# Layer 1's first expert: its rows by products from blocks on chip, its tables inside the first expert, and the overflow branch at each layer's end

## The chip, the cores and the metric

One core of a Trainium2 chip runs the kernel. The metric is device time in microseconds (us) of one execution. Engines: TensorE (PE, matrix products), VectorE (DVE), ScalarE (ACT), GpSimd (POOL) and SyncE (SP, which here issues loads).

## The reference

Two layers over 512 rows of width 1024. After a mixer and memory attention, each layer ends with an output projection, a norm and a grouped top-2 mixture of 16 experts:

```python
o = jnp.concatenate([tok, xa], axis=-1) @ w_out[i]
x = layer_norm(ALPHA * x + o, ln1_g[i], ln1_b[i])
f = grouped_moe(x, router_w, router_b, w_gate[i], w_up[i], w_down[i])
x = layer_norm(ALPHA * x + f, ln2_g[i], ln2_b[i])
...
scores = jax.nn.sigmoid(jnp.dot(xt.astype(jnp.float32), router_w.astype(jnp.float32)))
sel = scores + router_b.astype(jnp.float32)
...
for e in range(N_EXPERTS):
    h = jax.nn.silu(xt @ w_gate[e]) * (xt @ w_up[e])
    out = out + combine[:, e:e + 1] * (h @ w_down[e])
```

The group of four experts with the best sum of its two best `sel` is taken for each row, and in it the two best experts; `combine` holds their scores divided by their sum, and zero elsewhere.

## The kernel before

The 512 rows are four blocks of 128 (`xrow[0]` to `xrow[3]`, each 128 x 1024 on chip). Every large product is done as three (`mm3`, L202 to L204: high by high, high by low, low by high), so each operand is split into a high part, copied by ScalarE (L168), and a low part, a subtraction on VectorE (L169) or now and then on POOL. Weights come in pages of 1 MB through `W`: SP loads a raw page, the splits make high and low, and PE uses them; `W.keep`, `W.ahead` and `W.on_pool` say how many pages stay free, how far splits run ahead, and which of them POOL does.

The stage around the change, for each layer, is this. The output projection (`project_out`, products `oa`) is done column by column, one row block each, and each block goes through its norm (L458 to L466). `logits` stores the normed block to `x1d` and `rd` in HBM by POOL's queue, transposes it (products `rt`) and multiplies it with the router's weights (`lg`). `route` is a chain of some twenty small VectorE operations for blocks 0 to 2 together and then for block 3: ranks in the groups, the chosen group, `oh` (which experts a row goes to), and its place within each expert's list, which comes from PE counts (`pos`). With comparisons `sel` (0/1 matrices of 128 x 128, row by slot) `entries` multiplies a table `tok` of row numbers and gate factors into slots (`tab`); `tables` turns that into `idxs` (row number of each of 128 slots of each of 16 experts) and `gates`. `overflow` counts what doesn't fit in 128 slots (`cnt`, `ovf`, `nover`).

`experts` then gathers the rows of expert 0 and 1 from `x1d` by an indirect DMA of POOL (`xg`, L668), warms PE up (layer 1 only), runs `fill` (in layer 0 the keys and values of layer 1, `ka` and `va`, which hide the wait), and at `more` every engine loads `nover` (L893) and branches (L894) past the rare code for overfull experts. Then for each expert: transposes of the gathered rows (`xt`, split to `xgt`), `gate_up` (48 products `ga` and `ua` in two halves), an activation and a product (`h`), its transposes (`htr`, split to `ht`), and `down` (24 products `ya`), scaled by the gate and scattered into `rd`. Within the experts the order on PE, ScalarE and VectorE is that of the code (`manual_schedule`); before them, and at the last expert until its warm-up, a scheduler orders by its own costs. At the layer's end eight warm-up products, htr, four more, and the last expert's `ya` follow, whose result is added with `rd` for the second norm.

## Time and profile before

| | |
|---|---|
| median of three runs | 1035.75 us (1032.32 to 1035.86) |
| the profiled execution's own time | 1031.97 us, span 1030.1 us |
| mean granted TensorE clock | 0.973 |
| PE busy | 983.7 us, 95% of the span |
| VectorE, ScalarE, POOL busy | 774.2, 627.7, 200.5 us |
| time per expert in the steady part | 17.9 us |

The span goes from the first to the last instruction. PE is the engine that is busy nearly throughout; its idle stretches lie where a layer's experts begin. A granted clock of 1 is 2.4 GHz, 0.5 is 1.2 GHz.

### The profile page before, as it was taken

To read this page: it belongs to the slowest core of one execution; us is meant where nothing else is said; L and a number is where in the kernel's file an instruction comes from. 1 tells how busy PE (TensorE), PEld (TensorE's weight loads), DVE (VectorE), ACT (ScalarE), POOL (GpSimd) and SP (SyncE) were. 2 spreads that over 40 slices of the span, in tenths; PEclk is the share of its full clock that TensorE was granted. 3 is DMA by queue.
4 is the path that set the end of the run, shared out by engine and by line. 5 is a ranking of instruction groups with operands and counts; after the bars stand their busy time and mean duration, and the time that the engine had idled before them with its cause. 6 is when DMAs were issued, how large, how long until landed. Compare 5 with 4: busy or idle time off the path is not lost. (4 is left out here: it accounts for less than half of the span.)

```text
span 1030.1 us, 12721 instructions
## 1 busy us (share of the span) xinstructions
PE 983.7 (95%) x4815; PEld 810.6 (79%) x4816; DVE 774.2 (75%) x884; ACT 627.7 (61%) x684; POOL 200.5 (19%) x111
## 2 busy tenths in 40 slices
PE   8999999969999999999999999977899999999995
PEld 6788888858888888888679887865688888888873
DVE  4738567867989898898894455675689898988975
ACT  4626532556788787878643414233687887878763
POOL 0000002112332413321110000221133324233023
PEclk9999999989999999999999999987899999999998
DMA  9813266667999999999880425490799999999944
GB/s 321 294 42 123 91 237 247 244 225 265 364 367 333 366 360 360 360 357 362 282 320 1 164 82 207 131 396 25 232 330 362 372 327 383 359 362 355 357 87 160
DMA packets 102219, 273.30 MB, mean 265 GB/s; under 512 B 10442, under 2 KB 10966, under 8 KB 102152
## 3 DMA queue, kind: packets, MB, share of 16 engines
q1 hardware_dynamic: 89480, 242.84, 64.5%
q0 software_dynamic: 11808, 26.97, 9.4%
q10 hardware_dynamic: 864, 2.62, 0.7%
q8 instruction: 39, 0.64, 0.2%
q14 instruction: 28, 0.23, 0.1%
HBM read 262.22 MB, written 26.21 MB: 280 GB/s over the span
## 5 line engine op out<-in xcount | busy, mean ns | idle before, releaser
L169 DVE TENSOR_TENSOR low<-raw,high 128x2048 fp32r<-128x2048 f32 x189 | 427.9, 2288 | 80.9 <-ACT high L168 79.4
L168 ACT ACTIVATE high<-raw 128x2048 fp32r<-128x2048 f32 x189 | 355.1, 1910 | 22.7 <-PE ga L204 10.1
L668 POOL DMA_INDIRECT xg<-x1d,idxs x32 | 83.2, 2601 | 299.6 <-PE xt L677 270.5
L168 ACT ACTIVATE split<-raw 128x1024 fp32r<-128x1024 f32 x66 | 68.9, 1058 | 71.1 <-PE za L204 26.0
L202 PE MATMUL ya<-high,ht 128*128 128x512 f32 x256 | 103.8, 406 | 0.0
L169 DVE TENSOR_TENSOR split<-raw,split 128x1024 fp32r<-128x1024 f32 x61 | 73.6, 1221 | 39.6 <-ACT split L168 38.9
L204 PE MATMUL ga<-high,xgt 128*128 128x512 f32 x248 | 99.1, 399 | 2.9 <-DVE xgt L208 2.9
L204 PE MATMUL ya<-high,ht 128*128 128x512 f32 x256 | 101.3, 396 | 0.1
L203 PE MATMUL ya<-low,ht 128*128 128x512 f32 x256 | 101.1, 395 | 0.0
L202 PE MATMUL ga<-high,xgt 128*128 128x512 f32 x248 | 100.7, 406 | 0.1
L203 PE MATMUL ga<-low,xgt 128*128 128x512 f32 x248 | 98.4, 397 | 0.0
L204 PE MATMUL ua<-high,xgt 128*128 128x512 f32 x248 | 97.1, 392 | 0.0
L202 PE MATMUL ua<-high,xgt 128*128 128x512 f32 x248 | 96.9, 391 | 0.0
L203 PE MATMUL ua<-low,xgt 128*128 128x512 f32 x248 | 96.8, 390 | 0.0
L169 POOL TENSOR_TENSOR split<-raw,split 128x1024 fp32r<-128x1024 f32 x5 | 11.9, 2383 | 267.0 <-DVE sto L475 147.0
L202 PE MATMUL za<-xh,split 128*128 128x512 f32 x160 | 61.6, 391 | 2.0 <-ACT xh L207 2.0
L203 PE MATMUL za<-xl,split 128*128 128x512 f32 x160 | 62.5, 391 | 0.0
L204 PE MATMUL za<-xh,split 128*128 128x512 f32 x160 | 61.5, 389 | 0.0
L204 PEld LDWEIGHTS ga<-high,xgt 128*128 128x128 f32 x248 | 47.4, 191 | 14.1 <-DVE xgt L208 4.0
L204 PEld LDWEIGHTS ya<-high,ht 128*128 128x128 f32 x256 | 48.1, 188 | 12.8 <-DVE ht L208 1.3
L664 POOL DMA_INDIRECT rd<-h,idxs x16 | 40.4, 2523 | 89.3 <-ACT h L718 79.6
L202 PEld LDWEIGHTS ya<-high,ht 128*128 128x128 f32 x256 | 48.4, 189 | 10.5 <-ACT ht L207 0.6
(250 smaller groups left out, 1886.2 us busy)
## 6 DMA issues: line engine op xcount, KB each, us to landing
raw<-in_w_gate_dram SPq DMA_DIRECT2D x64, 1024.0 KB, 9.8
raw<-in_w_up_dram SPq DMA_DIRECT2D x64, 1024.0 KB, 9.6
raw<-in_w_down_dram SPq DMA_DIRECT2D x64, 1024.0 KB, 10.5
raw<-in_w_kv_dram SPq DMA_DIRECT2D x8, 1024.0 KB, 7.4
raw<-in_w_out_dram SPq DMA_DIRECT2D x8, 1024.0 KB, 8.0
raw<-in_w_in_b_dram SPq DMA_DIRECT2D x8, 1024.0 KB, 11.1
raw<-in_w_in_a_dram SPq DMA_DIRECT2D x6, 1024.0 KB, 5.4
x1d<-x POOLq DMA_DIRECT2D x8, 512.0 KB, 6.0
```

The lines of the kernel that those rows point to most:

```text
L168: act.activation(high, src, AF.Copy)
L169: (pool_e if self.on_pool(self.count) else vec).tensor_tensor(low, src, high, op=OP.subtract)
L202: pe.matmul(o, a[0], b[0], start=start, stop=False)
L203: pe.matmul(o, a[0], b[1], start=False, stop=False)
L204: return pe.matmul(o, a[1], b[0], start=False, stop=stop)
L664: added[e] = pool_e.indirect_dma_start(out=rd[i], out_offset=bass.IndirectOffsetOnAxis(ap=tabs[e][0], axis=0), in_=ys[e % 2], in_offset=No ...
L668: pool_e.indirect_dma_start(out=xg[:, e % 2], out_offset=None, in_=x1d[i], in_offset=bass.IndirectOffsetOnAxis(ap=tabs[e][0], axis=0), bou ...
```

## The change

Layer 0: the routing is cut into steps of a class (`choose`, `both`, `count`, `place`, `places`, `gates`). The lists of rows (`listed`, which makes `idxs`) are made apart from the gate factors (`weighed`). The two gathers are begun in the midst of the V products of `keys_values`, whose last half is put behind the list's last product. The gate factors and the overflow count (`rest`) follow, and the transposes of expert 0 come after the last V product.

Layer 1 (`mixer_end_dense`) has one written order from the output projection on. Expert 0 needs no list: 0/1 matrices `sel0` (row by slot of expert 0) are multiplied with the row blocks on chip (`first_rows`, 32 products `x0`), which gives its rows transposed. Four half pages of weights are split early and the others held back. The tables (`listed`, the gathers for experts 1 and 2) come after the first 12 products of expert 0, gate factors and overflow after the next 12. The norm of the last block is done in two halves, and the warm-up before the experts is gone.

Both layers: `more` (L958, L959) stands at the last expert, between its `gate_up` and the warm-up products, with a page of its own; one more page is kept free.

```diff
-    def keys_values(after=None):
+    def keys_values(begin=None):
...
         a = [acc("va") for _ in range(2)]
         for j in range(4):
+            if j == 2 and begin is not None:
+                begin()
             g = W.next()
             for kk in range(2):
                 k = 2 * j + kk
                 for m in range(2):
                     ms = slice(m * P, (m + 1) * P)
-                    with ExitStack() if after is None or j < 3 else tc.issue_after(after):
-                        mm3(a[m], (memh[:, k, ms], meml[:, k, ms]), (g[:, 0, kk, :], g[:, 1, kk, :]),
-                            k == 0, k == KB - 1)
+                    with ExitStack() if begin is None or j < 2 else tc.issue_after(last_listed[0]):
+                        end = mm3(a[m], (memh[:, k, ms], meml[:, k, ms]), (g[:, 0, kk, :], g[:, 1, kk, :]),
+                                  k == 0, k == KB - 1)
             W.done(g)
...
+        return kt, vt, end.ins
...
-    def entries(cs):
-
+    def chosen(sels=None, cs=range(NC)):
+
+        sels = page("sels", [P, NC, 2, P], FR) if sels is None else sels
         for c in cs:
-            if c == 0:
-                tab[:] = [tiny(3 * E, "tab")]
             for k in range(2):
-                m = pe.matmul(tab[0], choose(pos2[:, k, c:c + 1]), tok[:, c, k].rearrange("p e t -> p (e t)"),
-                              start=(c + k == 0), stop=(c + k == NC))
-        last_entry.append(m.ins)
-
-    def tables():
-
-        t = tab[0].rearrange("p (e t) -> p e t", t=3)
-        vec.tensor_scalar(idxs, t[:, :, 0], 1.0, None, op0=OP.subtract)
-        return vec.tensor_reduce(gates, t[:, :, 1:3], axis=AX.X, op=OP.add)
+                vec.tensor_scalar(sels[:, c, k], slot1, pos2[:, k, c:c + 1], None, op0=OP.is_equal)
+        return sels
+
+    def listed(sels, t=None, cs=range(NC)):
+
+        t = tiny(E, "rows") if t is None else t
+        for c in cs:
+            for k in range(2):
+                m = pe.matmul(t, sels[:, c, k], tok[:, c, k, :, 0], start=(c + k == 0), stop=(c + k == NC))
+        if NC - 1 in cs:
+            vec.tensor_scalar(idxs, t, 1.0, None, op0=OP.subtract)
+            last_listed[:] = [m.ins]
+        return t
+
+    last_listed = []
+
+    def weighed(sels):
+
+        t = tiny(2 * E, "gates").rearrange("p (e t) -> p e t", t=2)
+        for c in range(NC):
+            for k in range(2):
+                pe.matmul(t, sels[:, c, k], tok[:, c, k, :, 1:3], start=(c + k == 0), stop=(c + k == NC))
+        vec.tensor_reduce(gates, t, axis=AX.X, op=OP.add)
+        drop(sels)
 
...
-        def gate_up(e, between=None):
+        def gate_up(e, between=None, then=()):
             a = [acc("ga"), acc("ua")]
             for half in range(2):
                 if half and between is not None:
@@ -694,6 +756,8 @@
                         W.done(g)
                     if half and not u:
                         act.activation(hp[:, 0, :], a[0], AF.Silu)
+                    if 2 * half + u < len(then):
+                        then[2 * half + u]()
...
-        gather(0)
-        gather(1)
-        if i:
-            with tc.issue_after(last_entry[-1]):
-                keep_warm(8)
-        fill()
-        more(i, hy)
+        W.hold, W.ahead = False, 4
+        end = fill(lambda: begin(gather))
+        if not i:
+            rest()
         W.keep, W.flight = 0, 4
         W.ahead, W.whole, W.on_pool = 6, True, lambda n: False
         W.rings(8)
-        xtrans(0)
-        gather(2)
+        if not i:
+            with tc.issue_after(end):
+                xtrans(0)
+            gather(2)
+            order.enter_context(tc.manual_schedule(engines={ET.PE, ET.Activation, ET.DVE}))
         W.pump()
-        order = ExitStack()
-        order.enter_context(tc.manual_schedule(engines={ET.PE, ET.Activation, ET.DVE}))
         for e in range(E):
             if e == last:
                 order.close()
-            up = gate_up(e, (lambda: (down(last - 1, scaled(last - 1)), scatter(last - 1))) if e == last else None)
+            gate_up(e, (lambda: (down(last - 1, scaled(last - 1)), scatter(last - 1))) if e == last else None,
+                    (lambda: begin(gather), rest) if i and not e else ())
             if e + 1 < E:
                 xtrans(e + 1)
             if e + 3 < E:
...
             if e == last - 3:
-                W.keep = 4
+                W.keep = 5
...
+                spare = page("more", [P, 4, FE])
+                more(i, spare)
+                drop(spare)
...
         with tc.manual_schedule(engines={ET.PE, ET.Activation, ET.DVE, ET.Pool}):
-            with tc.issue_after(up.ins):
-                keep_warm(8)
+            keep_warm(8)
             htrans(last)
             keep_warm(4)
             down(last, parts)
...
+        for c0, n in ((0, 3), (3, 1)):
+            route.choose(c0, n, normed)
+            route.place(c0, n, route.count(c0, n))
+            route.both(c0, n)
+            route.places(c0, n)
+            chosen(sels, range(c0, c0 + n))
+            if c0 == 0:
+                listed(sels, t, range(n))
+        xt, xg = slots()
+
+        def begin(gather):
+            listed(sels, t, range(3, NC))
+            for e in range(2):
+                gather(e)
+
+        def rest():
+            route.gates()
+            weighed(sels)
+            overflow()
+        return xt, xg, begin, rest, ExitStack()
+
+    def mixer_end_dense(ch, cl, lnp):
+
...
+        W.hold = True
+        route = Router()
+        sel0 = page("sel0", [P, NC, P])
+        ready = y1[:, 0:1]
...
+        def choose_first(c):
+            vec.tensor_scalar(sel0[:, c], slot1, posp[:, c, 0:1], None, op0=OP.is_equal)
+
+        def first_rows(c, ks=range(KB)):
+
+            for k in ks:
+                k0 = 4 * P * (k // 4) + 2 * P * (k % 4 // 2) + k % 2
+                pe.matmul(rows0[k // 4][:, k % 4 * P:(k % 4 + 1) * P], xrow[c][:, k0:k0 + 2 * P - 1:2], sel0[:, c],
+                          start=(c == 0 and k % 4 == 0), stop=(c == NC - 1), skip_group_check=True)
+
+        order = ExitStack()
+        order.enter_context(tc.manual_schedule(engines={ET.PE, ET.Activation, ET.DVE}))
+        if True:
+            rows(0, column(0))
+            keep_rows(0, 1)
+            split()
+            split()
+            rows(1, column(1))
+            keep_rows(1, 1)
+            xts[0] = row_blocks(0)
+            split()
+            split()
+            rows(2, column(2, (3,), lambda j: logits(xts[0], route.of(0))))
+            keep_rows(2, 1)
+            xts[1] = row_blocks(1)
+            pos = []
+
+            def part(j):
+                if j == 3:
+                    logits(xts[1], route.of(1))
+                    route.choose(0, 2)
+                    act.activation(ready, ident[:, 0:1], AF.Sqrt)
+                else:
+                    pos.append(route.count(0, 2))
+                    route.place(0, 2, pos[0])
+                    choose_first(0)
+                    choose_first(1)
+            o = column(3, (3, 7), part)
+            rows(3, o, False)
+            keep_rows(3, 1)
+            rows0 = [acc("x0") for _ in range(2)]
+            xts[2] = row_blocks(2)
+            first_rows(0)
+            logits(xts[2], route.of(2))
+            route.choose(2, 1)
+            xts[3] = row_blocks(3)
+            first_rows(1, range(4))
+            logits(xts[3], route.of(3))
+            first_rows(1, range(4, KB))
+            pos.append(route.count(2, 1))
+
+            def third():
+                route.place(2, 1, pos[1])
+                choose_first(2)
+            route.choose(3, 1, None, third)
+            first_rows(2)
+            route.place(3, 1, route.count(3, 1))
+            choose_first(3)
+            first_rows(3)
+            drop(lnp, *xs)
+            xt, xg = slots()
+            route.both()
+            route.places()
+            for q in range(2):
+                split_to(xt[:, 0, 4 * q:4 * q + 4, :], xt[:, 1, 4 * q:4 * q + 4, :],
+                         rows0[q].rearrange("p (k s) -> p k s", s=P))
+            sels = chosen()
+        drop(sel0)
+
+        def rest():
+            route.gates()
+            weighed(sels)
+            overflow()
+
+        def begin(gather):
+            listed(sels)
+            for e in (1, 2):
+                gather(e)
+        return xt, xg, begin, rest, order
```

On VectorE in layer 0, the last rows of routing until the list: of before (`sel` are the comparisons, `split` and `low` weight splits, `tab` the table on PE):

```order
L587 TENSOR_REDUCE pos_99<-route_1582 128x2
L169 TENSOR_TENSOR split_1868<-raw_1225,split_1868 128x1024
L618 TENSOR_SCALAR sel<-slot_91,pos_99 128x128 x3
L169 TENSOR_TENSOR split_1883<-raw_1225,split_1883 128x1024
L618 TENSOR_SCALAR sel<-slot_91,pos_99 128x128 x2
L634 TENSOR_SCALAR idxs<-tab 128x16
L635 TENSOR_REDUCE gates<-tab 128x16
L169 TENSOR_TENSOR low_2081<-raw_1310,high_2080 128x2048
L169 TENSOR_TENSOR low_2057<-raw_1254,high_2056 128x2048
L208 TENSOR_TENSOR vt_1701<-va,vt_1701 128x512
L605 TENSOR_TENSOR ovf<-cnt,thr 1x48
L208 TENSOR_TENSOR vt_1701<-va,vt_1701 128x512
```

And of the change (`sels` are the comparisons, `rows` the list's table, L639 to L648 the gate factors, L657 to L662 the overflow count):

```order
L625 SCALAR_TENSOR_TENSOR posp<-pos,oh 128x16
L657 TENSOR_TENSOR ovf<-cnt,thr 1x48
L646 TENSOR_TENSOR route_1315<-route_1315 128x128
L633 TENSOR_TENSOR route_1315<-route_1315,posp 128x32
L660 TENSOR_REDUCE ovn<-ovf 1x1
L661 CAST flags<-ovf 1x48
L647 CAST tok<-route_1315 128x2x4x16
L634 TENSOR_REDUCE pos_99<-route_1315 128x2
L662 CAST nover<-ovn 1x1
L648 TENSOR_TENSOR tok<-route_1315,tok 128x2x4x16
L677 TENSOR_SCALAR sels_1580<-slot_91,pos_99 128x128 x2
L687 TENSOR_SCALAR idxs<-rows 128x16
```

Before, two splits stood among the comparisons, and the overflow count came after the list; now the gate factors' and the overflow count's operations stand among those of the list, ahead of it.

On VectorE at the end of layer 0's last expert, of before (`h` is the activation's product, `ht` the low part of its transposes, `yp` the last scaling):

```order
L169 TENSOR_TENSOR low_4222<-raw_4118,high_4221 128x2048
L693 TENSOR_TENSOR h_1692<-h_1692,ua 128x512
L169 TENSOR_TENSOR low_4241<-raw_4138,high_4240 128x2048
L208 TENSOR_TENSOR ht<-htr,ht 128x512
L169 TENSOR_TENSOR low_4259<-raw_4169,high_4258 128x2048
L775 SCALAR_TENSOR_TENSOR yp_4283<-ya,gates,yp_4283 128x512
```

And of the change, up to the load of `nover` that goes ahead of the branch:

```order
L169 TENSOR_TENSOR low_4069<-raw_3983,high_4068 128x2048
L755 TENSOR_TENSOR h_1651<-h_1651,ua 128x512
L169 TENSOR_TENSOR low_4088<-raw_4014,high_4087 128x2048
L169 TENSOR_TENSOR low_4106<-raw_4032,high_4105 128x2048
L958 TENSOR_LOAD nover
L959 COMPARE_AND_BRANCH
```

`ht` stood behind one `low` after `h`; now it comes behind two and the branch.

On VectorE in layer 1, within expert 0, of the change (L639 to L648 make the gate factors' entries, L699 `gates`):

```order
L208 TENSOR_TENSOR xgt_5864<-x_5747,xgt_5864 128x512
L208 TENSOR_TENSOR xgt_5864<-x_5748,xgt_5864 128x512
L677 TENSOR_SCALAR sels_5876<-slot_91,pos_99 128x128 x8
L169 TENSOR_TENSOR low_5895<-raw_5112,high_5894 128x2048
L169 TENSOR_TENSOR low_5917<-raw_5189,high_5916 128x2048
L687 TENSOR_SCALAR idxs<-rows 128x16
L169 TENSOR_TENSOR low_5951<-raw_5245,high_5950 128x2048
L639 TENSOR_TENSOR route_5518<-oh,route_5518 128x64
L641 TENSOR_REDUCE route_5518<-route_5518 128x4
L643 RECIPROCAL route_5518<-route_5518 128x4
L644 SCALAR_TENSOR_TENSOR route_5518<-route_5518 128x64
L646 TENSOR_TENSOR route_5518<-route_5518 128x128
```

In before, all of the routing stood ahead of the expert, and only `xgt` and four `low` up to `h`; PE's products `gates` now stand between the first 12 products of `ua` and the second half of `ga`.

## Rows read from the trace of the kernel before

**Rows 1.** Windows: length, busy PE, PEld, DVE, ACT, POOL; PE clock, DMA share, GB/s.

```profile
205.00:216.00 11.00, 3.60 (x19) 2.73 (x18) 6.77 (x9) 3.77 (x6) 1.61 (x3) 0.77 0.83 278
...
680.00:707.00 27.00, 15.75 (x91) 12.61 (x91) 19.39 (x73) 8.40 (x12) 7.29 (x6) 0.60 0.61 238
...
707.00:728.00 21.00, 16.33 (x69) 12.80 (x68) 14.76 (x11) 13.87 (x12) 2.06 (x2) 0.83 0.24 71
```

**Rows 2.** Timeline of VectorE (DVE), layer 0: start, length, idle before and its releaser.

```profile
179.02 1.28 DVE L466 SCALAR_TENSOR_TENSOR x<-x,rstd,ln 128x1024 f32<-128x1024 f32 x1
...
190.38 1.23 DVE L169 TENSOR_TENSOR split<-raw,split 128x1024 fp32r<-128x1024 f32 x1 [0.16 <-ACT split L168]
...
191.92 0.41 DVE L208 TENSOR_TENSOR kt<-ka,kt 128x256 fp32r<-128x256 f32 x1
...
195.21 0.67 DVE L618 TENSOR_SCALAR sel<-slot,pos 128x128 fp32r<-128x128 f32 x3
...
203.15 0.17 DVE L634 TENSOR_SCALAR idxs<-tab 128x16 int32<-128x16 f32 x1 [0.38 <-PE tab L627]
...
211.73 0.14 DVE L610 CAST nover<-ovn 1x1 int32<-1x1 f32 x1
```

**Rows 3.** Timeline of TensorE (PE), layer 0, first expert.

```profile
213.43 1.95 PE L677 MATMUL xt<-ident,xg 128*128 128x128 f32 x8 [7.40 <-DVEq L894]
...
215.22 0.80 PE L202 MATMUL ga<-split,xgt 128*128 128x512 f32 x1
```

**Rows 4.** Timeline, layer 1 before its first expert, several engines.

```profile
673.82 1.85 PE L525 MATMUL lg<-rw,x1t 128*128 128x16 f32 x16
...
678.73 0.39 PE L204 MATMUL oa<-split,cl 128*128 128x512 f32 x1
...
683.32 1.28 DVE L466 SCALAR_TENSOR_TENSOR x<-x,rstd,ln 128x1024 f32<-128x1024 f32 x1
...
686.06 3.60 PE L525 MATMUL lg<-rw,x1t 128*128 128x16 f32 x16
...
690.96 4.39 DVE L618 TENSOR_SCALAR sel<-slot,pos 128x128 fp32r<-128x128 f32 x3
...
693.47 1.80 POOL L655 MEMSET xg<- 128x2048 f32 x1 [0.23 <-DMA rd<-x]
...
696.68 0.18 DVE L549 SCALAR_TENSOR_TENSOR route<-route,before 128x16 f32<-128x16 f32 x1
...
704.48 0.13 DVE L610 CAST nover<-ovn 1x1 int32<-1x1 f32 x1
...
706.02 1.95 PE L677 MATMUL xt<-ident,xg 128*128 128x128 f32 x8 [2.12 <-PEq L894]
...
707.81 0.79 PE L202 MATMUL ga<-split,xgt 128*128 128x512 f32 x1
```

**Rows 5.** Timeline, layer 1, end of expert 0 and start of expert 1.

```profile
719.59 1.11 PE L677 MATMUL xt<-ident,xg 128*128 128x128 f32 x8
...
720.66 1.28 ACT L696 ACT_TABLE_LOAD   x1
...
724.21 1.11 PE L702 MATMUL htr<-ident,h 128*128 128x128 f32 x4 [3.51 <-DVE h L693]
...
727.33 0.80 PE L204 MATMUL ga<-high,xgt 128*128 128x512 f32 x1 [1.16 <-DVE xgt L208]
```

**Rows 6.** DMA issues: the gathers, median us from issue to landing.

```profile
xg<-x1d,idxs POOLq DMA_INDIRECT x32, 9.4
```

**Rows 7.** Timeline of VectorE, end of layer 0's last expert.

```profile
501.31 2.28 DVE L169 TENSOR_TENSOR low<-raw,high 128x2048 fp32r<-128x2048 f32 x1
...
503.51 0.68 DVE L208 TENSOR_TENSOR ht<-htr,ht 128x512 fp32r<-128x512 f32 x1
```

**Rows 8.** Timeline of VectorE, end of layer 1's last expert.

```profile
998.91 2.28 DVE L169 TENSOR_TENSOR low<-raw,high 128x2048 fp32r<-128x2048 f32 x1
...
1001.12 0.68 DVE L208 TENSOR_TENSOR ht<-htr,ht 128x512 fp32r<-128x512 f32 x1
```

More of the change, by code (lines that the diff above doesn't have):

```diff
@@ L502, in project_out @@
                 drop(ch[c // 2], cl[c // 2])
-            after(c, norm(xrow[c], st[c], lnp[:, 0], lnp[:, 1], D))
+            return norm(xrow[c], st[c], lnp[:, 0], lnp[:, 1], D, wide)
+        return column, rows
     posp = consts.tile([P, NC, E], FT, name="posp")
@@ new lines, in mixer_end, with split @@
+        xt, xg = slots()
[9 more added lines that the diff above has]
+    def mixer_end_dense(ch, cl, lnp):
+        column, rows = project_out(ch, cl, lnp)
+        W.keep, W.ahead = 7, 4
+        W.pump()
+        W.hold = True
+        route = Router()
+        sel0 = page("sel0", [P, NC, P])
+        ready = y1[:, 0:1]
+        xts = {}
+        def split():
+            if W.raw and len(W.ready) < 4 and free_pages:
+                W.split()
+        def choose_first(c):
[70 more added lines that the diff above has]
+        return xt, xg, begin, rest, order
@@ L1069, in trunk @@
+    rows = mixer_end(ch, cl, lnp)
     kv1 = []
```

209 lines of the change are left out of this document (118 added, 91 removed).

## The prediction

> **What bounds the kernel now.** I read the windows first [rows 1]. Over most of the span TensorE runs without a gap, so only stretches where it idles or runs at half clock can give anything back. Of those that this change touches, the window 205 to 216 us (start of layer 0's experts) shows 3.60 us of PE work in 11, at clock 0.77, and 680 to 707 us (layer 1, from the last norm to the first expert) shows 15.75 in 27 at clock 0.60. The window 707 to 728 (layer 1's first expert) has 16.33 in 21 at 0.83.
>
> Then the timeline of each place. In layer 0, VectorE makes the row list (idxs) at 203.15 [rows 2], and the first gathered transpose starts at 213.43 after 7.40 us idle [rows 3]. That idle ends with the branch, not the gather: the overflow count `nover` is there at 211.87 [rows 2] and PE starts 1.56 us later. In layer 1 the last w_out product ends at 679.12, the norm at 684.60; then VectorE routes alone, at half clock the sixteen lg products take 3.60 us instead of 1.85, `nover` ends at 704.61 and PE starts 1.41 us later, at 706.02 [rows 4]. In expert 0, ScalarE's splits and a table load (720.66) make the activation late: PE waits 3.51 us before htr and 1.16 before the third product of expert 1 [rows 5]. The gap before a third product means that the low half of its operand came last.
>
> **The change, part by part.** The sum is against the profiled execution's 1031.97 us (span 1030.1 and 1.9 around it).
>
> *Layer 0, start of the experts.* The V products of j = 2 and 3 (24 instructions of about 0.227 us, 5.44 in all) now stand behind the list, to cover the gather, and the branch is gone from here. What decides is when the list is ready. VectorE's new order has the ops of blocks 0 to 2 and of block 3 side by side, nine weight splits of 1.23 and the four kt halves [rows 2] among them, and six gate ops and the four overflow ops ahead of the last two sels. From the norm's end (180.3 [rows 2]) I count: four splits, the rate set by ScalarE as before, to 187.3; four route ops, a split and two more to 190.5; kt can't start before 191.92 [rows 2], so about 1.4 idle, then 1.3 for three of them; the remaining about 34 small ops at 0.13 to 0.2 and four splits to oh of block 3 at about 201.4; thirteen more (1.9) and six sels (1.35) to 204.7; eight ops and two sels to 206.8, the list at 207.4. That is 4.2 later than 203.15. PE, done with the first half of V at about 198, idles some 9 us; then the V rest takes 5.44 and about 2 more at half clock, as behind the idle of before (first products 0.80 instead of 0.39 [rows 3]): transposes at 214.8 and, 1.8 later as before, the first expert product at 216.6. That is 1.4 behind 215.22, but the five half-clock products of before there, about 1.0, are then paid. Net **+0.4**. Bounds: a list as early as before (203.15) gives 203.3 + 7.4 + 1.8 = 212.5, so −2.7 and with that 1.0 −3.7, and −5 if splits slip behind it; a gather that takes its median 9.4 us [rows 6] from 207.8 arrives at 217.2, 2.4 after the V products, and with one more us at half clock that gives +4. The gather is wanted 7 us after the list, so I take it as covered. The Trainium skill (DMA: Bandwidth & Descriptors, the fit for software-driven DMAs) has 2.0 us plus size over 436 GB/s, by which 512 KB would take an estimated 3.2 us; by that the gather is covered even with an early list, by the row only with luck.
>
> *Layer 0, end of the experts.* The branch (load of `nover`, compare) now stands between the last `ua` product and the warm-up products on every engine. PE loses the 1.41 to 1.56 us that it cost before [rows 2 to 4]. But VectorE's order is now h, low, low, branch, ht, where it was h, low, ht, low [rows 7]: the second low (2.28) and the branch stand in front of ht, so that ht starts near 501.31 + 2 × 2.2 + 1.4 = 507.1 instead of 503.51. The third product of `ya` waits for it, and the layer's end has nothing else for PE: **+3.5**. Bounds: if the raw page of that second low is late, the same or more, and if the clock falls in the wait, +5.5; if the low's partner on ScalarE were absent, the branch alone: +1.
>
> *Layer 1, start.* What goes: the table products, gather 0, the eight transposes, the warm-up of eight, the branch with its 1.41. What comes: 32 products of row blocks with sel0, of which 24 lie beside routing waits; the logits of block 1 and the counts of blocks 0 and 1 in the midst of column 3. Those hold column 3: lg 1.85 [rows 4], the rows of block 1, and a wait of about 0.95 for counts that VectorE finishes at 681.6. Last w_out product 682.6 (before 679.12). The norm then takes 4.9 (before 5.4, with a split in it): 687.5. Transposes of block 3, copies and lg to 691.6; about 16 dependent one-block route ops, 0.18 each [rows 4] and a little between them, give oh at 695.35; place, sel0 and the last eight products (1.85, priced as the lg row at full clock) end at 698.45. ScalarE's and VectorE's halves run beside: third `ga` product at 699.05, where before its first starts at 707.81: −9. POOL's 1.80 memset of xg now stands between the stores of blocks 2 and 3; in before, beside POOL's work up to the end of that memset at 695.27, VectorE took 4.39 for three sels that else take 0.67 [rows 2, 4]: VectorE hardly moves meanwhile. So it costs 0 to 1.8, and I take +1, on the counts or the norm.
>
> Inside expert 0 a part is given back. VectorE has, from 699.9: eight sels (1.75), two lows (4.6), idxs, a third low (2.3), seven gate ops (1.4): gate factors at about 710.2. PE finishes `ua`'s first half at 705.6 and the gates products wait in its queue ahead of `ga`'s second half: 4.6 idle, about 2 of half clock behind it. So xt of expert 1 starts at about 719, as in before (719.59). But by then the lows and the activation table are no longer behind: htr at about 720.4 instead of 724.21 and the third product of expert 1 at 723 instead of 727.33 [rows 5], with the half clock of before (0.83 in 707 to 728) gone. −5.3, and with the memset **−4.3**. Bounds: 0, if the gates wait costs half clock as long as before, and −9, if VectorE takes the gate ops before the lows' data are there.
>
> *Layer 1, end.* Here the order is h, branch, low, ht: h to 999.0, branch to 1000.4, low to 1002.7, ht against 1001.12 [rows 8]: **+1.5**, bounds +0.5 (the low's raw late on both sides) and +4.5 (clock falls).
>
> *The rest* I cost at nothing: page counts kept free (one load fewer in flight near the layers' ends, under a weight stock of several pages), the two half norms, and the extra table load, which ScalarE does in the shade of column 3.
>
> Sum: +0.4 + 3.5 − 4.3 + 1.5 = **+1.1**, 1033.1 by the profiled run. The four runs of before (1031.97 to 1035.86) have a mean of 1034.0, 2 above the profiled one; I put the prediction between, at **1034.0**.
>
> **Rivals.** What a measurement tells from no change is about 0.5%, 5.2 us.
>
> *Faster (a): the covers work.* The list comes as early as before (−3.7), the gate wait in expert 0 hides under `ua` (−8 with the memset), and the ends cost 3.5 + 1.5, or 2 if the second low of layer 0 doesn't count: −6.7 to −9.7, 1022 to 1025. For it speaks that the waits of the two windows [rows 1] add up to over 18 us of PE idle; against it VectorE's order with nine splits ahead of the list. Chance 0.34.
>
> *Slower (b): half clock at the ends and in the x0 stage.* After each idle of over 3 us PE's first products take 0.63 to 0.80 instead of 0.39 [rows 3, 5]. If the wait of 3.5 us at layer 0's end does this to its 24 `ya` products, at 0.2 each, that is 4.8: +1.1 + 4.8 = 5.9, 1038; with the same at layer 1's end (its high bound, 3 more) 1041, and with the x0 stage at half clock (4 more) 1045. The first decides: above no change from the point at which over 20 of the `ya` products run at half clock. For it speaks [rows 5], against it that four products of warm-up stand right ahead of `ya`. Chance 0.17.
>
> *Slower (c): the jump itself grows.* In before the branch took 1.56 at a DMA share of 0.83 [rows 1] and 1.41 in layer 1. If an engine's instructions behind the branch come by DMA behind the weight loads, the jump could take as long as a gather there (9.4 [rows 6]): up to 8 more at each end, from +1.1 to +17, 1049. The Trainium skill (Runtime: NRT & Kernel Launch, Instruction fetch mechanics) says that a taken branch out of the two pages held forces such a fetch before execution goes on. The trace bears this out only so far that each skip costs PE 1.41 to 1.56, fetch and load together, and the one at 0.83 speaks against a large size. Chance 0.07.
>
> *No change (d), the forecast.* Gain in layer 1 and loss at the ends cancel. Chance 0.42.
>
> **Numbers.** The likeliest case alone reaches from 1029 to 1038. From the bounds, low ends −5, +1, −9, +0.5 give 1019.5 and high ends +4, +5.5, 0, +4.5 give 1046; all at one end is unlikely, and with (a) taken in to 1021 (its 1022 and one more for the spread of single runs) and (b) to 1042 no more than 2 in 10 is left out: **1021 to 1042**. Faster by over 0.5%: (a) 0.34. Within: (d) 0.42. Slower: (b) and (c) 0.24.
>
> **What would show it.** In the profile after: idxs in layer 0 at 206 to 208, xt at 214 to 216; a VectorE low of 2.3 between h and ht at layer 0's end and `ya`'s third product 3 to 4 us after the second; in layer 1 the first `ga` 8 to 10 us earlier than 707.81, then a gap of 4 to 5 in front of the gates products, and htr about 4 earlier. I am wrong if the gates wait is absent (then faster), if PE's clock falls at the ends, or if the list in layer 0 comes at 203.

## The result and the profile after

The changed kernel takes 1041.64 us (median of four runs, 1041.11 to 1042.65) against 1035.47 (1032.32 to 1035.86) of the kernel before: ratio on record 1.0094, interval 1.0070 to 1.0118. The quotient of these two medians is only 1.0060; on another chip the same kernel (e5_changed below) has 1.0110 by its medians and a ratio of 1.0097. So it is slower by 0.6 to 1.1%, inside the range that was given, but the forecast was no change. The profiled execution takes 1042.65 us with a span of 1039.9, so 9.8 of span more than the profiled one of before (1031.97). The medians are 6.2 apart, so part of the 9.8 is the spread of single executions. The mean granted clock is 0.981, higher than before's 0.973.

To see where the 9.8 us come from, both spans are cut at PE rows that exist in either kernel: the last `oa` product of layer 0, the last expert's `xt`, the first `ra` of the layer's end, the first `oa` of layer 1, and again `xt` and `ra`. They start at 173.24, 476.51, 509.68, 631.16, 973.65 and 1007.10 before, and at 173.35, 481.95, 522.60, 646.86, 982.02 and 1016.97 after. Stage A holds layer 0's routing and experts, B its end, C the mixer of layer 1, D routing and experts of layer 1, E its end.

| us | A | B | C | D | E |
|---|---|---|---|---|---|
| before | 303.27 | 33.17 | 121.48 | 342.49 | 33.45 |
| after | 308.60 | 40.65 | 124.26 | 335.16 | 34.95 |
| difference | +5.33 | +7.48 | +2.78 | -7.33 | +1.50 |
| forecast | +0.4 | +3.5 | 0 | -4.3 | +1.5 |

The head (+0.11) and the tail (-0.07) make up the rest. The table is the scheme of all that follows: one stage came out as forecast, one gained more, three lost more. First the windows of the profile after, beside [rows 1], with the same columns:

```profile
205.00:216.00 11.00, 10.83 (x39) 9.16 (x40) 0.99 (x5) 3.42 (x2) 2.11 (x2) 0.64 0.39 121
216.00:227.00 11.00, 6.26 (x20) 4.63 (x20) 6.82 (x8) 4.15 (x6) 1.91 (x1) 0.69 0.95 361
501.00:516.00 15.00, 9.69 (x36) 6.04 (x35) 9.28 (x5) 6.71 (x6) 3.69 (x3) 0.79 0.78 237
680.00:712.00 32.00, 29.57 (x210) 26.37 (x209) 22.87 (x73) 9.34 (x18) 6.11 (x9) 1.00 0.83 294
712.00:732.00 20.00, 15.19 (x70) 12.43 (x70) 14.70 (x30) 9.68 (x7) 3.51 (x2) 0.83 0.79 282
```

The hole at 205 to 216 is filled, as meant: 10.83 us of PE instead of 3.60. But the next window has a hole of 4.7 us, and the end of layer 0 one of 5.3. In layer 1 the routing window, 15.75 of 27 at clock 0.60 before, is nearly full at clock 1.00, and the first expert has a new hole of 4.8.

**Start of layer 0's experts**, timelines of PE, VectorE and ScalarE (its last row) of the changed kernel, beside [rows 2, 3]:

```profile
215.37 1.20 PE L739 MATMUL xt<-ident,xg 128*128 128x128 f32 x8
217.81 0.50 PE L202 MATMUL ga<-split,xgt 128*128 128x512 f32 x1 [1.24 <-ACT xgt L207]
...
222.04 0.80 PE L204 MATMUL ga<-split,xgt 128*128 128x512 f32 x1 [3.50 <-DVE xgt L208]
222.63 0.63 PE L202 MATMUL ga<-split,xgt 128*128 128x512 f32 x1
...
205.17 1.43 PE L698 MATMUL gates<-tok,sels 128*128 128x32 f32 x6 [0.68 <-DVE tok L648]
...
207.26 0.17 DVE L687 TENSOR_SCALAR idxs<-rows 128x16 int32<-128x16 f32 x1 [1.85 <-PE rows L685]
215.60 2.29 DVE L169 TENSOR_TENSOR low<-raw,high 128x2048 fp32r<-128x2048 f32 x1 [8.16 <-PE gates L698]
...
217.91 2.28 DVE L169 TENSOR_TENSOR low<-raw,high 128x2048 fp32r<-128x2048 f32 x1
220.11 1.28 DVE L208 TENSOR_TENSOR vt<-va,vt 128x512 fp32r<-128x512 f32 x2
221.31 1.28 DVE L208 TENSOR_TENSOR xgt<-xt,xgt 128x512 fp32r<-128x512 f32 x2
...
212.58 3.72 ACT L168 ACTIVATE high<-raw 128x2048 fp32r<-128x2048 f32 x2 [12.91 <-PE va L204]
```

The list is there at 207.26 and the transposes start without a wait, so the gather is covered. Then VectorE does two whole lows and `vt` before it turns to `xgt`, the low half of the operand that PE's third `ga` product needs. ScalarE, too, makes two whole highs (to 216.30) ahead of the high half of `xgt`, for which PE's first product waits 1.24.

**End of layer 0**, PE and VectorE, beside [rows 7]:

```profile
511.35 3.60 PE L299 MATMUL warm<-ones_b 128*128 128x512 bf16 x8 [5.31 <-DVEq L959]
...
517.23 0.40 PE L203 MATMUL ya<-low,ht 128*128 128x512 f32 x1
...
506.14 0.69 DVE L755 TENSOR_TENSOR h<-h,ua 128x512 f32<-128x512 f32 x1 [0.46 <-PEq L959]
506.75 4.49 DVE L169 TENSOR_TENSOR low<-raw,high 128x2048 fp32r<-128x2048 f32 x2
516.47 0.69 DVE L208 TENSOR_TENSOR ht<-htr,ht 128x512 fp32r<-128x512 f32 x1 [5.23 <-ACT ht L207]
```

The last `ua` product starts at 505.65. PE's next instruction, the first behind the branch (L959), starts at 511.35, just after VectorE's second low ends at 511.24, and runs at half speed (eight warm-up products in 3.60 us).

**End of layer 1**, the same two engines, beside [rows 8]:

```profile
1007.99 1.90 PE L299 MATMUL warm<-ones_b 128*128 128x512 bf16 x8 [1.42 <-DVEq L959]
...
1007.03 0.69 DVE L755 TENSOR_TENSOR h<-h,ua 128x512 f32<-128x512 f32 x1 [1.07 <-PEq L959]
1008.21 2.29 DVE L169 TENSOR_TENSOR low<-raw,high 128x2048 fp32r<-128x2048 f32 x1 [0.49 <-DVEq L959]
1010.99 0.69 DVE L208 TENSOR_TENSOR ht<-htr,ht 128x512 fp32r<-128x512 f32 x1 [0.49 <-ACT ht L207]
```

The same branch, with no low between `h` and it on VectorE: PE waits 1.42 and the warm-up takes 1.90. The low behind the branch ends at 1010.50; `ht` comes 0.49 later, released by ScalarE.

**First expert of layer 1**, beside [rows 4, 5]:

```profile
713.37 0.48 PE L202 MATMUL ga<-split,xgt 128*128 128x512 f32 x1
...
725.13 1.89 PE L698 MATMUL gates<-tok,sels 128*128 128x32 f32 x8 [4.81 <-DVE tok L648]
...
727.56 0.63 PE L203 MATMUL ga<-low,xgt 128*128 128x512 f32 x1
...
735.79 0.66 PE L766 MATMUL htr<-ident,h 128*128 128x128 f32 x4
...
738.59 0.50 PE L204 MATMUL ga<-high,xgt 128*128 128x512 f32 x1 [1.68 <-DVE xgt L208]
...
716.45 4.50 DVE L169 TENSOR_TENSOR low<-raw,high 128x2048 fp32r<-128x2048 f32 x2
...
720.94 2.29 DVE L169 TENSOR_TENSOR low<-raw,high 128x2048 fp32r<-128x2048 f32 x1
...
724.74 0.33 DVE L648 TENSOR_TENSOR tok<-route,tok 128x128 fp32r<-128x128 f32 x1
```

Counted from stage D's start, the first `ga` is 66.5 us in (before 76.7), `htr` 88.9 (93.1), expert 1's third product 91.7 (96.2).

### The profile page after: what moved, and what is told of

Its sections match the earlier page's. It is cut to its first block, busy times and chain, and to the rows that moved or that the text cites. A ratio compares the mean times of both kernels' runs of the same rounds, so it can differ in the third digit from the quotient of the medians.

```text
span 1039.9 us, 12851 instructions
## 1 busy us (share of the span) xinstructions
PE 989.7 (95%) x4879; PEld 816.9 (79%) x4880; DVE 774.2 (74%) x889; ACT 626.4 (60%) x686; POOL 193.8 (19%) x106
## 5 line engine op out<-in xcount | busy, mean ns | idle before, releaser
L730 POOL DMA_INDIRECT xg<-x1d,idxs x31 | 85.9, 2771 | 304.1 <-PE xt L739 257.2
L169 DVE TENSOR_TENSOR split<-raw,split 128x1024 fp32r<-128x1024 f32 x65 | 78.5, 1221 | 41.5 <-ACT split L168 40.7
L203 PEld LDWEIGHTS ya<-low,ht 128*128 128x128 f32 x256 | 48.1, 188 | 10.7 <-DVE low L169 0.6
```

The costliest lines, as they stand in the source:

```text
L169: (pool_e if self.on_pool(self.count) else vec).tensor_tensor(low, src, high, op=OP.subtract)
L203: pe.matmul(o, a[0], b[1], start=False, stop=False)
L730: pool_e.indirect_dma_start(out=xg[:, e % 2], out_offset=None, in_=x1d[i], in_offset=bass.IndirectOffsetOnAxis(ap=tabs[e][0], axis=0), bou ...
```

## The experiments

All are edits of the changed kernel. Times are medians beside the kernel before on the same chip, ratio and interval are those on record and can differ from the quotient of the two medians; the stages come from each profile, cut as above.

| kernel | us | before | ratio, interval | A | B | C | D | E |
|---|---|---|---|---|---|---|---|---|
| e1_one | 1039.18 | 1030.70 | 1.0082, 1.0058 to 1.0106 | 306.55 | 37.78 | 124.45 | 334.22 | 34.92 |
| e1_none | 1040.14 | 1030.70 | 1.0063, 1.0033 to 1.0093 | 308.61 | 34.94 | 124.34 | 337.78 | 34.96 |
| e2_gates | 1039.91 | 1030.70 | 1.0082, 1.0060 to 1.0105 | 306.00 | 40.50 | 124.24 | 334.86 | 34.98 |
| e3_late | 1041.57 | 1030.70 | 1.0106, 1.0084 to 1.0128 | 306.51 | 40.49 | 124.24 | 334.43 | 34.93 |
| e5_changed | 1042.48 | 1031.11 | 1.0097, 1.0066 to 1.0128 | 307.24 | 40.50 | 124.22 | 334.94 | 34.93 |
| e6_order | 1035.47 | 1031.11 | 1.0034, 1.0016 to 1.0052 | 302.56 | 40.85 | 124.24 | 335.84 | 34.95 |
| e7_gates1 | 1034.79 | 1031.11 | 1.0024, 1.0006 to 1.0042 | 307.00 | 40.49 | 124.26 | 328.31 | 35.00 |
| e8_three | 1023.83 | 1031.11 | 0.9910, 0.9880 to 0.9941 | 302.09 | 34.91 | 124.37 | 331.09 | 34.95 |
| e9_back | 1028.55 | 1030.83 | 0.9978, 0.9961 to 0.9995 | 306.26 | 34.71 | 124.11 | 328.42 | 34.95 |
| e10_filler | 1049.58 | 1030.83 | 1.0186, 1.0154 to 1.0218 | 306.67 | 40.49 | 124.22 | 334.95 | 41.94 |
| e11_list | 1022.70 | 1031.69 | 0.9917, 0.9901 to 0.9934 | 300.11 | 34.95 | 124.36 | 329.71 | 34.96 |
| e12_three_again | 1023.28 | 1031.69 | 0.9925, 0.9907 to 0.9944 | 302.09 | 34.92 | 124.33 | 331.09 | 34.94 |

Where a stage was not touched it gives the spread: A 306.5 to 308.6, D 334.2 to 335.8 apart from e1_none (last section), and B, C and E within 0.4. The spread of A is that of TensorE's clock: of the 24 products of the V rest, whose code is the same, 6 (e1_one, e3_late) to 13 (the changed kernel's first profile, e1_none) ran at half speed.

**e1_one and e1_none: fewer lows ahead of layer 0's branch.** The stock of splits is held during the last expert's second half, so that one low, or none, stands between `h` and the branch on VectorE.

```diff
+                        if e == last and not i and half and u:
+                            W.hold = True
                         W.done(g)
...
             htrans(last)
+            W.hold = False
+            W.pump()
```

e1_none has the same lines without `and u`.

> The changed kernel with one of the two VectorE lows ahead of layer 0's branch put behind ht (its split is done in two halves there). In the changed kernel PE ends ua at 506.04, VectorE its two lows at 511.24, and PE's first warm-up product starts at 511.35, after 5.31 us idle. Theory A (the first PE instruction behind the branch waits for VectorE's last one ahead of it): the idle falls by one low, 2.25, to about 3.0; PE starts within 0.3 us of the low's end; whole time 2 to 4 us shorter, depending on the clock. Theory B (the jump itself takes 5.3 us, as its instructions come by DMA behind the weight loads): idle stays at 5.3, time within 1 us of the changed kernel.

> Both lows put behind ht, so that only h stands ahead of layer 0's branch on VectorE, as at layer 1's end. Theory A: idle about 1.4, as at layer 1's end (1.42), warm-up at full clock (1.90 instead of 3.60), the time 5 to 7 us below the changed kernel if the late splits hold nothing, and at least 4. Theory B: idle 5.3 as before, no gain, or a loss from the late splits.

Stage B goes down in steps with the lows: 40.65, 37.78, 34.94. Timelines at the branch, first e1_one (VectorE, then PE), then PE of e1_none:

```profile
506.66 2.28 DVE L169 TENSOR_TENSOR low<-raw,high 128x2048 fp32r<-128x2048 f32 x1
...
509.06 3.51 PE L299 MATMUL warm<-ones_b 128*128 128x512 bf16 x8 [3.11 <-DVEq L963]
```

```profile
509.34 1.90 PE L299 MATMUL warm<-ones_b 128*128 128x512 bf16 x8 [1.86 <-DVEq L963]
```

With one low PE starts 0.12 us after it ends (508.94), and the warm-up is at half speed; with none it waits 1.86 and the warm-up is at full speed. The median of e1_none gains less than its stage: its D is some 2.8 longer, from half clock in a stretch that the edit doesn't touch (last section), and the 5 to 7 us below the changed kernel that were expected don't show in it.

**e10_filler: more work ahead of the branch in layer 1,** where the wait is short. Four small products of VectorE are put there.

```diff
+                if i:
+                    for k in range(4):
+                        vec.tensor_tensor(spare[:, k], hp[:, 1, :], hp[:, 1, :], op=OP.mult)
                 more(i, spare)
```

> The changed kernel with four products of 128x512 (results unused) on VectorE ahead of layer 1's branch, behind h; one weight low (2.29) comes ahead of the branch too. Nothing else moves there. Theory A (PE's first instruction behind the branch waits for VectorE's last ahead of it): PE's idle before the warm-up grows from 1.42 by about 2.5 + 2.2 to 6, with PE starting within 0.3 us of the low's end and the warm-up at half clock (3.6 instead of 1.9): 4 to 7 us slower than the changed kernel. Theory B (fetch of instructions): idle stays at 1.4, and only the htr is later by VectorE's work, 0 to 3 us.

VectorE and PE of e10_filler:

```profile
1007.18 2.50 DVE L829 TENSOR_TENSOR more<-h 128x512 f32<-128x512 f32 x4
1009.59 2.29 DVE L169 TENSOR_TENSOR low<-raw,high 128x2048 fp32r<-128x2048 f32 x1
...
1011.99 3.59 PE L299 MATMUL warm<-ones_b 128*128 128x512 bf16 x8 [6.00 <-DVEq L962]
```

The four products moved a low ahead of the branch too, so it is a load of 4.7 us. PE starts 0.11 after it ends, the warm-up is again at half speed, and E grows by 7.0. The wait at the branch can thus be made at will on another engine, in the layer where it was short.

**e2_gates: the V products behind the gate products.** It tells whether the two lows wait for PE's last gate product, as the row at 215.60 names it.

```diff
...
+            route.gates()
+            last_listed[:] = [weighed(sels).ins]
...
         def rest():
-            route.gates()
-            weighed(sels)
             overflow()
```

> The changed kernel with layer 0's V rest put behind the last gates product (0.2 us of PE) rather than behind the list's. Theory C (at the start of layer 0's experts the third ga product waits 3.50 us because VectorE's two weight lows, held 8.16 us by the gates product that PE had queued behind the V rest, come between the gathered rows and their low half): the lows run beside the V rest, the low half of xgt is ready some 4 us earlier, the 3.50 wait goes and with it most of the half clock behind it (products of 0.63 from 222 to 226): 4 to 6 us shorter. Rival D (the late list, 207.26 against 203.15, and the half clock of the V rest are the loss): within 1 us of the changed kernel.

VectorE of e2_gates:

```profile
215.44 4.49 DVE L169 TENSOR_TENSOR low<-raw,high 128x2048 fp32r<-128x2048 f32 x2 [7.08 <-PE va L204]
```

The gate products are done at 208.12 and the lows come at 215.44 all the same, released by the V products, whose last page is done there. A is 306.0, half a us below the untouched ones. The gate product is not the cause; what is left is the order, lows ahead of `vt` and `xgt`.

**e6_order: the written order begins ahead of expert 0's transposes,** so that no scheduler puts the lows in front of `vt` and `xgt`.

```diff
         if not i:
+            order.enter_context(tc.manual_schedule(engines={ET.PE, ET.Activation, ET.DVE}))
             with tc.issue_after(end):
...
-            order.enter_context(tc.manual_schedule(engines={ET.PE, ET.Activation, ET.DVE}))
```

> The changed kernel with only the order at the start of layer 0's experts changed: the gathered rows' halves (xgt) come before the first two whole weight splits on ScalarE and VectorE. Theory C2 (the low half of xgt is late because it stands behind two lows whose pages the V rest frees only at its end): the third ga product comes 4 us earlier, its 3.5 us wait and the half clock behind it go: 4 to 6 us shorter than the changed kernel, if the later lows do not stop ga's second half. Rival D (late list and half clock of the V rest): within 1 us.

PE and VectorE of e6_order:

```profile
217.44 0.50 PE L202 MATMUL ga<-split,xgt 128*128 128x512 f32 x1 [0.21 <-ACT xgt L207]
...
217.45 1.28 DVE L208 TENSOR_TENSOR xgt<-xt,xgt 128x512 fp32r<-128x512 f32 x2
219.71 6.69 DVE L169 TENSOR_TENSOR low<-raw,high 128x2048 fp32r<-128x2048 f32 x3 [0.97 <-ACT high L168]
```

No wait before the third product, none of the half clock behind it, and A is 302.56: 0.7 below before, 6.0 below the changed kernel's first profile and 4.7 below e5_changed, its profile on the same chip. The last is the like comparison, as eight V products ran at half speed in both. The edit moves ScalarE's highs behind `xgt`, too, so the 4.7 are those of both engines' order.

**e3_late and e7_gates1: the gates of layer 1.** e3_late puts `rest` one step later in expert 0. e7_gates1 makes the gate operations right behind the sels and holds the splits until the list is made.

```diff
-                    (lambda: begin(gather), rest) if i and not e else ())
+                    (lambda: begin(gather), lambda: None, rest) if i and not e else ())
```

```diff
-        W.hold, W.ahead = False, 4
+        W.hold, W.ahead = bool(i), 4
...
             sels = chosen()
+            route.gates()
...
         def rest():
-            route.gates()
             weighed(sels)
...
                 gather(e)
+            W.hold = False
+            W.pump()
```

> The changed kernel with layer 1's gate factors and overflow count one quarter later in expert 0, behind the second 12 ga products. Theory E (PE's wait of 4.81 us before the gates products, with the half clock of 726.99 to 731.6 behind it, gives back what the start of layer 1 gained): the wait goes, the 12 ga products take 2.7 instead of 4.9 us: 5 to 7 us shorter. Rival F (VectorE's lows in expert 0 hold the next thing in line, h and xgt, just as long): the wait moves to htr or to expert 1's third product, 0 to 2 us.

> The changed kernel with layer 1's gate factor operations right behind the sels on VectorE, and the three weight lows of expert 0 held until after the list's. Theory E2 (it is the three lows, 6.8 us, ahead of the gate factors that make PE wait 4.81 before the gates products): the wait goes, the second ga half runs at full clock: 5 to 7 us shorter than the changed kernel. Rival F (the lows then hold ga's second half as long): a new wait of 3 to 5 us there and 0 to 2 us in all.

VectorE and PE of e3_late, then of e7_gates1:

```profile
718.54 4.48 DVE L169 TENSOR_TENSOR low<-raw,high 128x2048 fp32r<-128x2048 f32 x2
...
724.91 1.52 PE L698 MATMUL gates<-tok,sels 128*128 128x32 f32 x8 [4.29 <-DVE tok L648]
```

```profile
720.03 6.70 DVE L169 TENSOR_TENSOR low<-raw,high 128x2048 fp32r<-128x2048 f32 x3
...
721.64 0.96 PE L698 MATMUL gates<-tok,sels 128*128 128x32 f32 x8
```

Given more time, VectorE took one more low ahead of the gate operations, and the wait only moved (D 334.43). Given the order, the wait is gone and D falls by 6.9 to 328.31; now PE waits 1.68 us for a gather ahead of expert 1's transposes (729.95), which the longer wait had hidden.

**e5_changed** is the changed kernel once more, beside e6_order to e8_three. **e8_three** has the edits of e1_none, e6_order and e7_gates1 together, and **e12_three_again** is the same. In e5_changed the three waits came at 5.32, 3.26 and 4.84 us, as expected.

> The changed kernel again, as the yardstick on the chip of the next three. Every theory: 0.9 to 1.2% slower than before, with PE idle 5.31 at layer 0's end, 3.50 before the third ga product of layer 0 and 4.81 before layer 1's gates products, each within 0.3.

> All three together: no low ahead of layer 0's branch, xgt first at the start of layer 0, layer 1's gate factors first. If theories A, C2 and E2 hold and add up: 14 to 18 us below the changed kernel, so 0.3 to 0.8% faster than before. If gains in one place are given back at another (weights late, as the loads are DMA bound in the steady part): no better than before.

> The three corrections again, beside the run with the list first. Every theory: 0.7 to 1.1% faster than before, as on the other chip (0.991).

The three add up: the median is 18.7 below that of e5_changed, a little more than the 14 to 18 expected. Stage by stage A, B and D of the single edits come back (D 2.8 longer, half clock in the `x0` products again), and the kernel is 0.8 to 0.9% faster than before.

**e9_back: layer 0's branch back ahead of its experts,** with the edits of e6_order and e7_gates1; layer 1's stays at the end.

```diff
             rest()
+            more(i, hy)
...
-                spare = page("more", [P, 4, FE])
-                more(i, spare)
-                drop(spare)
+                if i:
+                    spare = page("more", [P, 4, FE])
+                    more(i, spare)
+                    drop(spare)
```

> The kernel with all three corrections, but layer 0's branch back ahead of its experts (behind the V products) instead of held lows at the layer's end. The end of layer 0 (last transposes of expert 15 to the first ra product) should take 33.2 us as before, against 34.9 with the branch there and no low ahead of it: 1.7 less. At the start PE's first transpose waits for VectorE's last operation ahead of the branch, the second half of vt, some 2 us behind the last V product, where it waited for nothing: 2 to 4 more. Theory A therefore: 0 to 3 us slower than all three together. If a branch in the shade of the gather is free: 1 to 2 us faster. The 2.8 us that the mixer of layer 1 took longer in every kernel so far goes if the branch at layer 0's end or the page kept for it is its cause, and stays otherwise.

VectorE and PE of e9_back:

```profile
216.77 0.68 DVE L208 TENSOR_TENSOR vt<-va,vt 128x512 fp32r<-128x512 f32 x1
...
218.24 1.33 PE L739 MATMUL xt<-ident,xg 128*128 128x128 f32 x8 [2.14 <-DVEq L961]
219.64 0.80 PE L202 MATMUL ga<-split,xgt 128*128 128x512 f32 x1
...
507.87 0.66 PE L766 MATMUL htr<-ident,h 128*128 128x128 f32 x4 [0.85 <-DVE h L755]
```

There PE's first instruction behind the branch is the transpose, 0.8 after VectorE's `vt` ends, and the first products run at half speed: A is 4.2 longer than in e8_three. B, 34.71, doesn't fall to before's 33.17 although no branch is left there. The trace shows where the 1.5 us go: nothing holds the eight warm-up products behind `ua` any more, they run at 493.77 ahead of expert 14's `ya`, and PE waits 0.85 us before `htr` and 0.72 before the third `ya` product. Of the whole, e9_back keeps 0.2% of gain over before where the three corrections had 0.8 to 0.9%; by their medians it is some 5 us behind e8_three, more than the 0 to 3 expected.

**e11_list: e8_three with the list's last operations ahead of the gate operations.**

```diff
-            vec.tensor_scalar(idxs, t, 1.0, None, op0=OP.subtract)
+            made[:] = [vec.tensor_scalar(idxs, t, 1.0, None, op0=OP.subtract).ins]
...
         def rest():
-            route.gates()
+            with tc.issue_after(made[0]):
+                route.gates()
```

> All three corrections, and layer 0's gate factors moved on VectorE from ahead of the list to behind it; the eight gates products on PE then stand between the V rest and the transposes instead of ahead of the list. VectorE has seven operations (1.4 us with their gaps) less before the list and PE six gates products (1.4) less: the list 1.5 to 3 us earlier after the last w_out product than with the three corrections (about 33.6). Against it eight gates products (1.5 to 1.9) ahead of the transposes. If the list bounds this stage: 0 to 1.5 us shorter than the three corrections; if the gather or the transposes do, the same or up to 2 us longer.

VectorE of e11_list, then of e12_three_again:

```profile
205.30 0.17 DVE L687 TENSOR_SCALAR idxs<-rows 128x16 int32<-128x16 f32 x1 [0.49 <-PE rows L685]
```

```profile
209.29 0.17 DVE L687 TENSOR_SCALAR idxs<-rows 128x16 int32<-128x16 f32 x1 [1.85 <-PE rows L685]
```

Counted from each kernel's last `oa` product (173.46 and 175.36) the list is 2.1 us earlier and A 2.0 shorter. The medians, 0.6 us apart, don't tell the two kernels apart.

## Why the prediction was wrong, step by step

The sum was +1.1 and the span grew by 9.8. What failed, stage by stage:

**Layer 0's start, +0.4 against +5.3.** The list (207.4 forecast, 207.26 measured) and the transposes (214.8, 215.37) came within 0.6 us. For the list this is in part luck: VectorE had its last `sels` at 205.41, 1.4 before the 206.8 of the sum, and then waited 1.85 for PE, where six gate products (205.17, 1.43) that the sum doesn't have stood ahead of the list's last. The V rest was priced 0.9 too short, as 13 of its 24 products ran at half speed. The step that failed is "1.8 later as before, the first expert product": it took the way from `xt` to the products over from before, where no low and no `vt` stood between. From `xt` to the first `ua` product it is 11.1 us, before 5.8: 1.24 of wait at the first product, 3.50 at the third and the half clock behind it. These 5.3 and the 1.8 by which `xt` is later make 7.1; 1.9 come back in expert 1, where the products behind a wait of 1.71 ran at half speed before and those behind 1.68 run at full speed after. Now the pages that the V rest frees release two lows just when `xt` starts, and a scheduler, not the written order, rules there. e6_order takes this away and A ends at -0.7 to before, near the +0.4. The gather was taken as covered, and it was: the gathers issued at 205 to 220 land in a median 4.0 us, not the 9.4 of [rows 6]. The fit of the Trainium skill (DMA: Bandwidth & Descriptors, Anatomy of one DMA — SWDGE (gpsimd) path) gave an estimated 3.2, and here the trace is nearer to it than to the row over the whole span.

**Layer 0's end, +3.5 against +7.5.** VectorE's order (h, low, low, branch, ht) was read rightly, and its lows are the price. But the step "ht starts near 507.1, and the third product of `ya` waits for it" named the wrong waiter. Nothing was priced for PE's own way over the branch beyond 1.4; in fact PE starts nothing behind the branch until VectorE has finished what stands ahead of it. So both lows go into PE's wait in full: the warm-up starts 29.4 us after `xt` where it started 23.9 after it before, and from the warm-up to `ra` it is 11.25 instead of 9.24, at half clock first. 5.5 and 2.0 make the 7.5. PE's row of before:

```profile
500.44 1.90 PE L299 MATMUL warm<-ones_b 128*128 128x512 bf16 x8
```

e1_one, e1_none and e10_filler show it in both directions. What stays without any low, +1.8 in e1_none, is inside the +1 to +5.5 given.

**Layer 1's start, -4.3 against -7.3.** The mechanism was right: the wait at the gates (4.6 forecast, 4.81 measured), `htr` (3.8 earlier forecast, 4.1 measured) and expert 1's third product (4.3 and 4.4). Two terms were mis-sized. The half clock that goes was put at about 1.0 (the -5.3 less the 4.3), but from that product to the next `xt` before took 13.3 us and after takes 10.6 (738.59 to 749.19), 2.7 less. Before, the clock is 0.50 from `htr` (724.21, behind the wait of 3.51) to 731; after, where 1.68 ahead of that product is the only wait since `xt`, it is 1.00. And the memset, taken at +1, cost nothing to be seen: VectorE's routing operations beside it take 0.17 to 0.29 each as they do without it, and `oh` of block 3 is there 63.3 after the stage's start, where the sum without the memset had 64.2. These 1.7 and 1.0 make most of the missing 3.0. POOL's row after:

```profile
694.92 1.83 POOL L1109 MEMSET xg<- 128x2048 f32 x1
```

The wait that remained, at the gates, was VectorE's order, too, as e7_gates1 shows.

**Layer 1's end, +1.5 against +1.5.** The size is right, and the branch alone, with no low ahead of it, is its cause. The path isn't the one of the sum, which let `ht` come late behind VectorE's low: the wait is PE's own 1.42 at the branch, and `ht` waits for ScalarE's half, not for the low (1010.99). That both paths give 1.5 is luck; at layer 0's end, with the same step, they don't.

**The rest, 0 against +2.8.** In layer 1's mixer, C is 124.1 to 124.5 in every variant and 121.48 before; e9_back rules out the branch and its page at layer 0's end. The trace shows one more weight split on VectorE amid the norm at the layer's end: four there now, three before, each about 1.17. VectorE's row after, then before's:

```profile
541.51 2.31 DVE L169 TENSOR_TENSOR split<-raw,split 128x1024 fp32r<-128x1024 f32 x2
```

```profile
528.36 1.18 DVE L169 TENSOR_TENSOR split<-raw,split 128x1024 fp32r<-128x1024 f32 x1
```

That PE is 1.3 us late by the first products `sc`, some 40 us into the stage, and loses as much again up to `oa`, where a wait of 0.84 for VectorE's `pt` (646.06) is new, fits this, but no run shows that the split is the cause. Nor was it tried why the splits run earlier; the page kept free, which moves when splits may start, is the suspect, no more.

**The rivals.** Half clock at the ends (b) is nearest in its time (1038 to 1045), but not in its place: it asked for over 20 of the 24 `ya` products at half clock, and these run at full speed (0.39 or 0.40) from the second, at 517.23, on; it is the wait and the warm-up. (a), the covers, needed a list as early as before and a hidden wait at the gates, and had neither; only the gather was covered. That e8_three, with the order mended, is 7.3 below before, inside the 6.7 to 9.7 of (a), comes by other terms: A is 1.2 shorter instead of 3.7, and D 11.4 instead of 8, against +2.9 in C that nobody had. (c), the jump itself growing by up to 8 us, falls. By the Trainium skill (Runtime: NRT & Kernel Launch, Instruction fetch mechanics) a taken branch out of the held pages costs a fetch before execution goes on; at DMA shares of 0.80 to 0.95 around these branches PE started 0.11 to 0.12 us after VectorE's last low, with one low or two, so no fetch is to be seen beyond that wait. Within the 1.42 and 1.86 us that stay without a low, the load, the jump and a fetch can't be told apart here.

## What to carry to other kernels

Moving a branch moves a meeting point: ask what each other engine still has in its queue ahead of it, since PE's wait here was that queue's length and not the price of the jump. When a change covers a wait, follow the operand behind it to the third product: what frees pages during the cover also releases splits, and unless the order puts them behind it these come first. Three such orderings, worth 5 to 7 us each, were the difference between 0.9% slower and 0.9% faster.

## What the runs showed of the hardware

A branch that every engine takes held PE for 1.42 (layer 1) and 1.86 us (layer 0, e1_none) with nothing behind `h` ahead of it on VectorE, 3.11 with one low, 5.31 with two and 6.00 with four small products and a low. Behind the waits of 3.5 to 5.3 us in the changed kernel PE's granted clock was 0.50 (222.0 to 226.5, 727.0 to 731.4 and 511.3 to 514.7): its products took 0.63 instead of 0.39, and a wait cost some 2 us more than its length.

The same code can also run at either level without a longer wait ahead of it. The sixteen `x0` products behind a wait of 0.82 us (their row reads `x<-sel,x`) took 2.15 us in the changed kernel and 3.53 in e8_three:

```profile
708.63 2.15 PE L1174 MATMUL x<-sel,x 128*128 128x128 f32 x16 [0.82 <-DVE sel L1168]
```

```profile
699.98 3.53 PE L1178 MATMUL x<-sel,x 128*128 128x128 f32 x16 [0.82 <-DVE sel L1172]
```

The code of this place is the same in all thirteen profiles of the changed kernel and its variants. Five (e1_none, e6_order, e8_three, e11_list, e12_three_again) show 3.5 to 3.6 us there, the other eight 2.15. The clock had already fallen: the five us from 691.6 of e8_three have 0.66, those from 695.0 of e9_back, the same place, 1.00, with PE as busy in the five us before (4.42 and 4.47 us). D is longer by 2.8 in e8_three for it (331.09 against 328.31 of e7_gates1), by 1.4 in e11_list. The edits of the five have nothing in common that reaches this place, other than that it comes at another time, and one kernel need not behave alike each time: the five executions of e1_none took 1035.11, 1035.55, 1040.14, 1040.39 and 1040.71 us, at a mean granted clock of 0.986 in the first two and 0.980 in the others. The profile is of the 1040.14; where the two short ones ran faster, no profile shows. What sets it off wasn't found.
